# A decoder trunk on one core: the inverse's input blocks stored straight from the masked scores, their norms as four rows of a matmul, and v centred by the matmul that turns it

## The chip, the core and the metric

The kernel runs on one core of one Trainium2 chip. A core has a matrix engine (PE, whose weight loads are listed as PEld), a vector engine (DVE), a scalar engine (ACT), GpSimd (POOL) and SyncE (SP), which in this kernel does nothing but issue transfers. The transfers run on 16 DMA engines. Every engine works off its own queue in order, and semaphores hold one back for another. The metric is device microseconds for one execution; lower is better.

## What is computed

A layer of RWKV-7 time mixing, then a layer of differential attention, for a sequence of 1024 tokens and a width of 1024. All of it is float32. The change lies in the first layer, of which this part matters:

```
kk = hd(k * k_k);  kk = kk / max(sqrt(sum(kk*kk, -1)), 1e-12)     # 16 heads of 64
kmod = hd(k * (1 + (a - 1) * k_a));  decay = exp(-exp(hd(w)))
step:  sa    = state @ (-kk_t)
       state = state * decay_t + sa x (kk*ah)_t + v_t x kmod_t
       y_t   = state @ r_t
mean = mean(y, -1);  var = mean((y - mean)**2, -1)
yn = (y - mean) * rsqrt(var + GN_EPS) * ln_w + ln_b
o  = (yn + sum(rh*kmod*r_k) * vh) * silu(g)
```

The mean of y over a head is taken away by taking the mean of v over the head away beforehand, since y is linear in v.

## The kernel before, in words

**Layer one** replaces the scan over tokens by chunks of 64 tokens. A unit of work, M, is two chunks of eight heads (four pairs of heads); there are 16 of them. Each goes through these steps: `prep` (decays, the scaled k, r and a, and the masked products `pm` of every token with every other in its chunk), `invert` (the unit lower triangular system of each block of 32 tokens, by substitution on POOL), `merge` (two blocks of 32 become one of 64), `chain` (the state is carried through the two chunks) and `norm`. In the steady part, slot i runs `chain` of M[i], `norm` of M[i-1], `merge` of M[i+1], `invert` of M[i+2] and `prep` of M[i+3], with the projections of the layer (`proj_step`: 24 matmuls of 512 columns for one pair of heads and half the tokens, weights `wf` split into `wh` and `wl`) put between as filling.

**From the scores to the inverse.** `prep` writes `pm` in four DVE instructions (L502). A block of 32 tokens wants 31 rows of `pm` and, as its row 31, the squared norms of k. Before the change, a matmul (L475) with the 128x128 constant `last` sums the squares `sq` and puts the norms on every partition that is the last of a block and zero on the others; four ACT copies (L485) bring it to the tile `ab`; four DVE additions (L510) add the rows of `pm`; and one transfer (L511) stores `ab` to DRAM as `dA`, laid out [8 chunks, 4 blocks, 32 rows, 32]. A second transfer (L528) reads `dA` back as `al`, one block per partition, four times over. `invert` then takes `ni` from row 31 of `al` (L538, L539), scales `al` (L540) on DVE, starts `xx` (L542, L545) and runs 31 steps of two POOL instructions (L551, L553). The result goes out as `dX` (L556) and comes back as `qd` (L558), which `merge` turns (L576).

**v.** When `proj_step` makes v (p is 2), its result `ev` is turned by four PE transposes per step (L211), DVE sums each head (L215) and takes the mean away while it evicts (L217), and L220 stores it as `d_vc`. There are 16 such steps: eight with the first half of the tokens, early on, and eight with the second half, at the start of the steady part.

**What sets the order.** The order in which instructions stand on each engine is not the program's: a planner runs through the program with durations of its own (`Durations`) and priorities (`PRI`), and lays each engine's queue out accordingly, for layer one and the first six steps of layer two. So a change at one place can move instructions everywhere. Transfers are all issued on SP's one queue.

Of the kernel before, what the change touches and what calls it, by code (L numbers as in the profile page):

```python
# [11 lines left out]
F32 = mybir.dt.float32  # L12
# [3 lines left out]
ALU = mybir.AluOpType  # L16
AX = mybir.AxisListType
# [3 lines left out]
P = 128  # L21
# [3 lines left out]
C = 64  # L25
# [51 lines left out]
class Trunk:  # L77
# [10 lines left out]
    def start(self, lp, xnT):  # L88

        nc, tc, I = self.nc, self.tc, self.I  # L90
        const = self.const
        self.ident = const.tile([P, P], F32, name="ident")
        make_identity(nc, self.ident)
        self.par = const.tile([P, len(ROWS), KT], F32, name="par")
        self.mug = const.tile([P, 6, KT], F32, name="mug")
# [13 lines left out]
        for t0 in range(0, KT, 2):  # L109
            ms = lp.tile([P, 2], F32, name="ms")  # L110
            for i in range(2):
                sq = lp.tile([P, D], F32, name="sq", bufs=1)
# [3 lines left out]
            for i in range(2):  # L116
# [5 lines left out]
                for hf in range(2):  # L122
                    pt = self.fps.tile([P, 4, P], F32, name="fl")
# [36 lines left out]
    def proj_step(self, hf, p, pr, src, group):  # L160

        nc, I = self.nc, self.I
        sl = slice(hf * TH, (hf + 1) * TH)
        G = {"w": []}
# [31 lines left out]
        def post(k):  # L196
# [11 lines left out]
            if k == 2:  # L208
                G["pt"] = pt = self.fps.tile([P, 4, P], F32, name="fl")
                for i in range(4):  # L210
                    nc.tensor.transpose(out=pt[:, i, :], in_=G["ev"][:, i * P:(i + 1) * P], identity=self.ident)  # L211
            if k == 4:
                ptv = G["pt"].rearrange("p i (h e) -> p (i h) e", e=64)
                mn = self.evp.tile([P, 8], F32, name="mn")
                nc.vector.tensor_reduce(mn, ptv, axis=AX.X, op=ALU.add)  # L215
                vc = self.evp.tile([P, 4, P], F32, name="ev")
                nc.vector.scalar_tensor_tensor(vc.rearrange("p i (h e) -> p (i h) e", e=64),  # L217
                                               mn.unsqueeze(2).to_broadcast([P, 8, 64]), -1.0 / 64, ptv,
                                               op0=ALU.mult, op1=ALU.add)
                nc.sync.dma_start(out=self.d_vc[sl, pr * P:(pr + 1) * P].rearrange("(i p) e -> p i e", p=P), in_=vc)  # L220
# [174 lines left out]
    def wkv_open(self):  # L395
        nc, tc = self.nc, self.tc
# [26 lines left out]

        self.last = cst.tile([P, P], F32, name="last")
        nc.gpsimd.memset(self.last, 0.0)
        for o in (0, 64):
            nc.gpsimd.memset(self.last[o:o + 64, o + 31:o + 64:32], 1.0)
        self.omka = cst.tile([P, KT], F32, name="omka")
# [14 lines left out]
    def prep(self, M, following):  # L443
# [29 lines left out]
        nc.vector.tensor_tensor(ae, ae, em, op=ALU.mult)  # L473
        nps = ps.tile([P, 8, C], F32, name="sc")
        nc.tensor.matmul(nps.rearrange("p c t -> p (c t)"), lhsT=self.last, rhs=sq.rearrange("p u t -> p (u t)"), start=True, stop=True)  # L475
        yield 0
# [5 lines left out]

        ab = tp.tile([P, 8, 32], F32, name="ab")
        for b in range(4):
            nc.scalar.copy(out=ab[32 * b:32 * b + 32], in_=nps[32 * b:32 * b + 32, :, b % 2 * 32:b % 2 * 32 + 32])  # L485
        nc.gpsimd.tensor_tensor(bk[:, :, 1, :], ch(kmod), em, op=ALU.mult)
# [21 lines left out]
        for b in range(4):  # L508
            bs = slice(32 * b, 32 * b + 32)
            nc.vector.tensor_tensor(ab[bs], ab[bs], pm[bs, b // 2, :, b % 2 * 32:b % 2 * 32 + 32], op=ALU.add)  # L510
        nc.sync.dma_start(out=dA.rearrange("c x s t -> (x s) c t"), in_=ab)  # L511
        yield 0
# [217 lines left out]
    def layer1(self):  # L730
# [11 lines left out]
        self.xmp = st.enter_context(tc.tile_pool(name="xmp", bufs=XB, side="right", reuse_waits="tile"))  # L742
        self.evp = st.enter_context(tc.tile_pool(name="evp", bufs=2, side="right", reuse_waits="tile"))

        def src_of(hf):
# [592 lines left out]
```

## Time and profile before

| | us |
|---|---|
| median of 3 runs (1627.41 to 1634.28) | 1633.85 |
| the profiled execution | 1635.44 |
| its span, first to last instruction | 1633.6 |
| PE busy | 1494.4 (91%) |
| DVE busy | 1194.8 (73%) |
| ACT busy | 909.6 (56%) |
| POOL busy | 672.8 (41%) |

A row of the windows view gives, for each stretch, the length of time in which each engine was busy, the granted TensorE clock as a share of 2.4 GHz, the mean busy share of the 16 DMA engines (packets overlap on an engine, so it can be over 1) and what they moved. A row of the lines view is a group of equal instructions: line, engine, operation, what is written from what, shape, count, then busy time in us and the mean of one in ns, then the idle time just before them. In the timeline, a row is start, length, engine, line, operation and, in brackets, the idle time before it and what ended it; SPq is SP's queue, and there the length is that of the issue, not of the transfer. In the chain, a row is start, length and what.

### The profile page before, as it was taken

To read this page: it belongs to the slowest core of one execution; us is meant where nothing else is said; L and a number is where in the kernel's file an instruction comes from. 1 tells how busy PE (TensorE), PEld (TensorE's weight loads), DVE (VectorE), ACT (ScalarE), POOL (GpSimd) and SP (SyncE) were. 2 spreads that over 40 slices of the span, in tenths; PEclk is the share of its full clock that TensorE was granted. 3 is DMA by queue.
4 is the path that set the end of the run, shared out by engine and by line. 5 is a ranking of instruction groups with operands and counts; after the bars stand their busy time and mean duration, and the time that the engine had idled before them with its cause. 6 is when DMAs were issued, how large, how long until landed. Compare 5 with 4: busy or idle time off the path is not lost.

```text
span 1633.6 us, 31095 instructions
## 1 busy us (share of the span) xinstructions
PE 1494.4 (91%) x10496; PEld 1208.3 (74%) x10496; DVE 1194.8 (73%) x3119; ACT 909.6 (56%) x2095; POOL 672.8 (41%) x1685
## 2 busy tenths in 40 slices
PE   3799999988998999979869789999999999999897
PEld 3577777666776777768758567788888888888786
DVE  7745658866879798788555777887878888787764
ACT  5645565745657586655234644665565656556420
POOL 4000003856878688778656111233232333333100
PEclk8799999989999999979879789999999999999999
DMA  7654677755656567656446451211111111113231
GB/s 195 187 185 144 186 226 216 201 163 152 194 157 175 164 179 190 185 160 174 128 142 164 131 169 58 67 46 31 46 46 27 46 33 40 40 40 119 92 126 52
DMA packets 218095, 207.39 MB, mean 127 GB/s; under 512 B 78032, under 2 KB 163280, under 8 KB 217936
## 3 DMA queue, kind: packets, MB, share of 16 engines
q1 hardware_dynamic: 217936, 205.40, 42.9%
q8 instruction: 83, 1.36, 0.3%
q14 instruction: 76, 0.62, 0.1%
HBM read 147.09 MB, written 58.27 MB: 126 GB/s over the span
## 4 chain that ended last, share of the span: by engine, by line
PE 63%; DVE 14%; DMA 7%; ACT 6%; issue 5%; POOL 4%; SPq 1%; ACTq 0%; DVEq 0%; POOLq 0%
PE pj L878 6%; PE pj L877 6%; PE pj L879 6%; PE fl L192 5%; PE fl L193 5%; PE fl L194 5%; PE tr L982 4%; PE sc L940 2%; PE sc L941 2%; PE tr L970 2%; POOL xx L553 2%; POOL tm L551 2%; DMA al<-dA 1%; PE sc L498 1%; PE tr L1255 1%
## 5 line engine op out<-in xcount | busy, mean ns | idle before, releaser
L192 PE MATMUL fl<-xh,wh 128*128 128x512 f32 x512 | 212.2, 420 | 11.2 <-DVE ev L217 8.8
L877 PE MATMUL pj<-wh,xh 128*128 128x512 f32 x512 | 214.1, 418 | 0.0
L193 PE MATMUL fl<-xl,wh 128*128 128x512 f32 x512 | 209.2, 410 | 3.7 <-DVE xl L151 3.7
L553 POOL TENSOR_TENSOR xx<-xx,tm 128x60 f32<-128x60 f32 (+24 forms) x496 | 196.8, 397 | 36.4 <-DVE xx L545 0.4
L194 PE MATMUL fl<-xh,wl 128*128 128x512 f32 x512 | 209.3, 410 | 0.0
L551 POOL TENSOR_TENSOR tm<-al,xx 128x60 f32<-128x60 f32 (+24 forms) x496 | 190.2, 383 | 40.4 <-DVE xx L545 4.0
L878 PE MATMUL pj<-wh,xl 128*128 128x512 f32 x512 | 202.7, 396 | 2.6 <-DVE xl L1216 2.6
L879 PE MATMUL pj<-wl,xh 128*128 128x512 f32 x512 | 202.1, 396 | 0.0
L157 DVE TENSOR_TENSOR wl<-wf,wh 128x512 fp32r<-128x512 f32 x160 | 119.0, 748 | 80.4 <-ACT wh L156 79.5
L946 ACT ACTIVATE p<-sc,mx 128x256 f32<-128x256 f32 (+7 forms) x128 | 94.6, 741 | 142.1 <-DVE mx L945 123.1
L926 POOL CAST kh<-kh 64x128 fp32r<-64x128 f32 x128 | 45.2, 353 | 263.4 <-ACT kh L918 250.0
L156 ACT CAST wh<-wf 128x512 fp32r<-128x512 f32 x160 | 97.6, 617 | 94.1 <-PE fl L193 71.6
L192 PEld LDWEIGHTS fl<-xh,wh 128*128 128x128 f32 x512 | 98.4, 192 | 40.3 <-issue 12.4
L193 PEld LDWEIGHTS fl<-xl,wh 128*128 128x128 f32 x512 | 99.0, 193 | 29.2 <-DVE xl L151 5.2
L194 PEld LDWEIGHTS fl<-xh,wl 128*128 128x128 f32 x512 | 98.7, 193 | 24.0 <-issue 1.4
L879 PEld LDWEIGHTS pj<-wl,xh 128*128 128x128 f32 x512 | 96.8, 189 | 21.9
L878 PEld LDWEIGHTS pj<-wh,xl 128*128 128x128 f32 x512 | 97.5, 190 | 19.6 <-DVE xl L1216 4.3
L877 PEld LDWEIGHTS pj<-wh,xh 128*128 128x128 f32 x512 | 97.5, 190 | 15.4 <-ACT xh L1215 0.2
L944 DVE TENSOR_REDUCE mx<-sc 128x1 f32<-128x256 f32 (+7 forms) x128 | 95.4, 753 | 0.8
L982 PEld LDWEIGHTS tr<-v,p 128*128 128x128 f32 x576 | 74.9, 194 | 7.8 <-ACT p L972 3.2
L982 PE MATMUL tr<-v,p 128*128 128x128 f32 x576 | 76.1, 278 | 2.1 <-ACT p L972 2.1
L940 PE MATMUL sc<-kh,q 128*128 128x512 f32 (+2 forms) x192 | 70.9, 378 | 4.0 <-issue 2.1
(295 smaller groups left out, 3695.3 us busy)
## 6 DMA issues: line engine op xcount, KB each, us to landing
wf<-in_a_w_in SPq DMA_DIRECT2D x64, 512.0 KB
d_in<-ev SPq DMA_DIRECT2D x64, 256.0 KB
wf<-in_b_w SPq DMA_DIRECT2D x64, 256.0 KB
xk<-d_xn SPq DMA_DIRECT2D x40, 256.5 KB
al<-dA SPq DMA_DIRECT2D x16, 512.0 KB
wf<-in_a_w_out SPq DMA_DIRECT2D x16, 512.0 KB
p<-d_x SPq DMA_DIRECT2D x10, 512.0 KB
d_c<-cc SPq DMA_DIRECT2D x16, 260.0 KB
```

The lines of the kernel that those rows point to most:

```text
L156: self.nc.scalar.copy(out=wh, in_=wf)
L157: self.nc.vector.tensor_tensor(wl, wf, wh.bitcast(F32), op=ALU.subtract)
L192: nc.tensor.matmul(G["ps"], lhsT=wh[:, kk, :], rhs=xh, start=(k == 0), stop=False)
L193: nc.tensor.matmul(G["ps"], lhsT=wh[:, kk, :], rhs=xl, start=False, stop=False)
L194: nc.tensor.matmul(G["ps"], lhsT=wl[:, kk, :], rhs=xh, start=False, stop=(k == KT - 1))
L551: nc.gpsimd.tensor_tensor(tv, al[:, s:s + 1, s + 1:].to_broadcast([P, n, w]), xx[:, 0:n, s:s + 1].to_broadcast([P, n, w]), op=ALU.mult)
L553: nc.gpsimd.tensor_tensor(xx[:, 0:n, s + 1:], xx[:, 0:n, s + 1:], tv, op=ALU.add)
L877: nc.tensor.matmul(pf, lhsT=self.X[i][0][:, k], rhs=wh, start=(k == 0), stop=False)
L878: nc.tensor.matmul(pf, lhsT=self.X[i][1][:, k], rhs=wh, start=False, stop=False)
L879: nc.tensor.matmul(pf, lhsT=self.X[i][0][:, k], rhs=wl, start=False, stop=(k == KT - 1))
L940: nc.tensor.matmul(sc[:, b:e], lhsT=q[:, m], rhs=H["kh"][:, m, b:e], start=True, stop=False)
L982: nc.tensor.matmul(po, lhsT=at[:, b, :], rhs=H["v"][:, b, :], start=(b == 0), stop=(b == i))
```

## The change

There are two edits.

**The substitution's input.** `last` goes; a constant `pick` [128, 2, 4] takes its place, and two accumulating matmuls with four weight columns each give the norms as four rows, one for each block of a chunk, [4, 8, 32]. One ACT copy brings them to an `ab` of four partitions, and a transfer of its own stores them as row 31 of each block. The four DVE additions go. The rows 0 to 30 of each block go to DRAM from `pm` itself, in four transfers, each of 31 partitions, 8 chunks and 32 numbers. So five transfers take the place of one, with as many runs of 128 bytes in all, and `al` waits for all five.

**v centred.** A constant `less` (the identity less 1/64 in each head's block) takes the place of the identity in the four PE instructions per step, which become matmuls. What they write is centred already, so the sum and the subtraction on DVE give way to one DVE copy.

```
+        nc.gpsimd.tensor_tensor(self.less, self.less, self.ident, op=ALU.add)
...
-                    nc.tensor.transpose(out=pt[:, i, :], in_=G["ev"][:, i * P:(i + 1) * P], identity=self.ident)
+                    nc.tensor.matmul(pt[:, i, :], lhsT=G["ev"][:, i * P:(i + 1) * P], rhs=self.less, start=True, stop=True)
...
-                mn = self.evp.tile([P, 8], F32, name="mn")
-                nc.vector.tensor_reduce(mn, ptv, axis=AX.X, op=ALU.add)
...
-                nc.vector.scalar_tensor_tensor(vc.rearrange("p i (h e) -> p (i h) e", e=64),
-                                               mn.unsqueeze(2).to_broadcast([P, 8, 64]), -1.0 / 64, ptv,
-                                               op0=ALU.mult, op1=ALU.add)
+                nc.vector.tensor_copy(out=vc, in_=G["pt"])
...
-        nps = ps.tile([P, 8, C], F32, name="sc")
-        nc.tensor.matmul(nps.rearrange("p c t -> p (c t)"), lhsT=self.last, rhs=sq.rearrange("p u t -> p (u t)"), start=True, stop=True)
+        nps = ps.tile([P, 8, C], F32, name="sc")[0:4, :, 0:32]
+        for b in range(2):
+            nc.tensor.matmul(nps, lhsT=self.pick[:, b, :], rhs=ch(sq)[:, :, b * 32:b * 32 + 32], start=b == 0, stop=b == 1)
...
-        ab = tp.tile([P, 8, 32], F32, name="ab")
-        for b in range(4):
-            nc.scalar.copy(out=ab[32 * b:32 * b + 32], in_=nps[32 * b:32 * b + 32, :, b % 2 * 32:b % 2 * 32 + 32])
+        ab = tp.tile([4, 8, 32], F32, name="ab")
+        nc.scalar.copy(out=ab, in_=nps)
+        nc.sync.dma_start(out=dA[:, :, 31, :].rearrange("c x t -> x c t"), in_=ab)
...
         for b in range(4):
-            bs = slice(32 * b, 32 * b + 32)
-            nc.vector.tensor_tensor(ab[bs], ab[bs], pm[bs, b // 2, :, b % 2 * 32:b % 2 * 32 + 32], op=ALU.add)
-        nc.sync.dma_start(out=dA.rearrange("c x s t -> (x s) c t"), in_=ab)
+            bs = slice(32 * b, 32 * b + 31)
+            nc.sync.dma_start(out=dA[:, b, 0:31, :].rearrange("c s t -> s c t"), in_=pm[bs, b // 2, :, b % 2 * 32:b % 2 * 32 + 32])
```

SP's queue around the seventh unit's store of `dA` and its reading back, before; a row is line, operation, what is written from what, and the shape on the written side:

```order
L556 DMA dX<-xx 4x256x32
L204 DMA d_in_61<-ev 128x512
L168 DMA wf<-in_a_w_in 128x1024
L558 DMA qd<-dX 128x8x32
L511 DMA dA<-ab 128x8x32
L528 DMA al<-dA 128x1x1024
L441 DMA a<-d_a 128x4x128
L526 DMA d_bv<-v 128x512
L204 DMA d_in_61<-ev 128x512
L168 DMA wf<-in_a_w_in 128x1024
```

The same place on SP after the change:

```order
L205 DMA d_in_61<-ev 128x512
L169 DMA wf<-in_a_w_in 128x1024
L554 DMA dX<-xx 4x256x32
L509 DMA dA<-pm 31x8x32 x4
L556 DMA qd<-dX 128x8x32
L526 DMA al<-dA 128x1x1024
L438 DMA a<-d_a 128x4x128
L205 DMA d_in_61<-ev 128x512
L169 DMA wf<-in_a_w_in 128x1024
L524 DMA d_bv<-v 128x512
```

The one store of 128 partitions has become four of 31, which here also stand ahead of the reading of `qd`; the store of the norms (not in these rows) stands further up, and what stood behind the reading of `al` still does.

DVE's queue from the last two masks `pm` of the seventh unit on, before (`ni`, L538, stands 34 rows behind the last mask):

```order
L502 TENSOR_TENSOR pm<-sc,pmask 128x512 x2
L510 TENSOR_TENSOR ab<-ab,pm 32x256 x3
L651 COPY uv<-zu 64x4x64
L510 TENSOR_TENSOR ab<-ab,pm 32x256
L686 TENSOR_SCALAR ve<-mg 128x8
L157 TENSOR_TENSOR wl<-wf,wh 128x512
L68 TENSOR_SCALAR gn_t<-ve 128x8
```

The same place on DVE after the change:

```order
L501 TENSOR_TENSOR pm<-sc,pmask 128x512 x2
L158 TENSOR_TENSOR wl<-wf,wh 128x512
L649 COPY uv<-zu 64x4x64
L479 TENSOR_TENSOR bk<-kraw,a 64x8x64
L480 TENSOR_TENSOR bk<-kraw,a 64x8x64
L684 TENSOR_SCALAR ve<-mg 128x8
```

The additions are gone, and `ni` (L536 now) stands 27 rows behind the last mask where it stood 34 rows behind.

## Rows read from the trace of the kernel before

**Rows 1.** windows: busy us of PE, PEld, DVE, ACT, POOL; clock, DMA, GB/s

```profile
100.00:250.00 150.00, 147.94 (x662) 116.87 (x661) 88.16 (x130) 89.14 (x160) 9.88 (x28) 1.00 0.62 194
250.00:750.00 500.00, 460.75 (x4277) 355.43 (x4276) 394.63 (x852) 311.00 (x631) 367.11 (x842) 0.94 0.63 177
750.00:900.00 150.00, 124.82 (x1578) 110.92 (x1577) 91.82 (x266) 62.90 (x132) 92.82 (x254) 0.89 0.54 151
```

**Rows 2.** timeline of SP's queue at the seventh unit's store and reading

```profile
471.36 0.56 SPq L556 DMA_DIRECT2D dX<-xx  x1
...
476.30 0.37 SPq L558 DMA_DIRECT2D qd<-dX  x1
478.29 0.37 SPq L511 DMA_DIRECT2D dA<-ab  x1
480.51 0.56 SPq L528 DMA_DIRECT2D al<-dA  x1
...
486.02 0.46 SPq L168 DMA_DIRECT2D wf<-in_a_w_in  x1
```

**Rows 3.** timeline: DVE and POOL where `al` is first used

```profile
453.39 0.18 DVE L538 TENSOR_SCALAR ni<-al 128x32 f32<-128x32 f32 x1 [5.17 <-DMA al<-dA]
...
495.14 0.29 DVE L538 TENSOR_SCALAR ni<-al 128x32 f32<-128x32 f32 x1
...
471.41 0.24 POOL L551 TENSOR_TENSOR tm<-al,xx 128x31 f32<-128x31 f32 x1
```

**Rows 4.** waits: engine, line, waited for: us in total, times, longest

```profile
SPq L558 <- DMA dX<-xx: 13.3, 11, 4.3
...
SPq L528 <- DMA dA<-ab: 7.8, 5, 3.3
...
DVE ni L538 <- DMA al<-dA: 11.9, 5, 5.2
```

**Rows 5.** by line: issues of two stores, ns min/median/max, first and last start

```profile
L511 SPq DMA_DIRECT2D dA<-ab x16: 370/371/2242, 257.0 to 812.3; - x16
...
L556 SPq DMA_DIRECT2D dX<-xx x16: 533/564/572, 309.3 to 886.7; - x16
```

**Rows 6.** windows: the last `dA` and the last `dX` on their way

```profile
813.20:814.00 0.80, 0.80 (x35) 0.63 (x33) 0.60 (x3) 0.00 (x0) 0.62 (x3) 1.00 1.04 164
...
888.00:890.70 2.70, 2.70 (x46) 2.50 (x45) 1.89 (x10) 0.95 (x2) 0.47 (x1) 1.00 0.34 48
```

**Rows 7.** chain that ended last: start, us, what; two readings of `al`

```profile
261.26 10.69 DMA al<-dA
...
441.36 12.01 DMA al<-dA
```

**Rows 8.** timeline of SP's queue: the issue behind a store of `dX`

```profile
588.77 0.57 SPq L556 DMA_DIRECT2D dX<-xx  x1
589.44 2.18 SPq L168 DMA_DIRECT2D wf<-in_a_w_in  x1
```

**Rows 9.** lines: what goes on DVE and ACT, and a copy

```profile
L510 DVE TENSOR_TENSOR ab<-ab,pm 32x256 f32<-32x256 f32 x64 | 26.9, 421 | 0.9
...
L485 ACT COPY ab<-sc 32x256 f32<-32x256 f32 x64 | 23.2, 362 | 3.9 <-PE sc L475 3.2
...
L215 DVE TENSOR_REDUCE mn<-fl 128x8 f32<-128x512 f32 x16 | 11.0, 689 | 11.0 <-PE fl L211 10.9
...
L217 DVE SCALAR_TENSOR_TENSOR ev<-mn,fl 128x512 f32<-128x512 f32 x16 | 10.9, 681 | 6.0 <-DMA d_vc<-ev 5.8
...
L129 DVE COPY xnT<-fl x8: 677/684/692, 16.5 to 63.1; 128x512 f32<-128x512 f32 x8
```

**Rows 10.** lines on PE: old norms, old turn (100 to 250 us), a matmul

```profile
L475 PE MATMUL sc<-sq,last 128*128 128x512 f32 x32 | 16.8, 605 | 0.2 <-ACT sq L467 0.2
...
L211 PE MATMUL fl<-ident,ev 128*128 128x128 f32 x32 | 4.9, 275 | 0.5 <-ACT ev L203 0.5
...
L982 PE MATMUL tr<-v,p 128*128 128x128 f32 x406 | 52.7, 275 | 0.0
```

More of the change, by code (lines that the diff above doesn't have):

```diff
@@ L210, in post @@
                 for i in range(4):
-                    nc.tensor.transpose(out=pt[:, i, :], in_=G["ev"][:, i * P:(i + 1) * P], identity=self.ident)
+                    nc.tensor.matmul(pt[:, i, :], lhsT=G["ev"][:, i * P:(i + 1) * P], rhs=self.less, start=True, stop=True)
             if k == 4:
-                ptv = G["pt"].rearrange("p i (h e) -> p (i h) e", e=64)
-                mn = self.evp.tile([P, 8], F32, name="mn")
-                nc.vector.tensor_reduce(mn, ptv, axis=AX.X, op=ALU.add)
                 vc = self.evp.tile([P, 4, P], F32, name="ev")
-                nc.vector.scalar_tensor_tensor(vc.rearrange("p i (h e) -> p (i h) e", e=64),
-                                               mn.unsqueeze(2).to_broadcast([P, 8, 64]), -1.0 / 64, ptv,
-                                               op0=ALU.mult, op1=ALU.add)
+                nc.vector.tensor_copy(out=vc, in_=G["pt"])
                 nc.sync.dma_start(out=self.d_vc[sl, pr * P:(pr + 1) * P].rearrange("(i p) e -> p i e", p=P), in_=vc)
@@ L422, in wkv_open @@
         nc.gpsimd.memset(self.bones[64:P, 64:P], 1.0)
[L424 to L427, printed above, removed]
+        self.pick = cst.tile([P, 2, 4], F32, name="pick")
+        nc.gpsimd.memset(self.pick, 0.0)
+        for h in range(2):
+            for b in range(2):
+                nc.gpsimd.memset(self.pick[h * 64:h * 64 + 64, b, 2 * h + b:2 * h + b + 1], 1.0)
         self.omka = cst.tile([P, KT], F32, name="omka")
@@ L473, in prep @@
         nc.vector.tensor_tensor(ae, ae, em, op=ALU.mult)
-        nps = ps.tile([P, 8, C], F32, name="sc")
-        nc.tensor.matmul(nps.rearrange("p c t -> p (c t)"), lhsT=self.last, rhs=sq.rearrange("p u t -> p (u t)"), start=True, stop=True)
+        nps = ps.tile([P, 8, C], F32, name="sc")[0:4, :, 0:32]
+        for b in range(2):
+            nc.tensor.matmul(nps, lhsT=self.pick[:, b, :], rhs=ch(sq)[:, :, b * 32:b * 32 + 32], start=b == 0, stop=b == 1)
         yield 0
@@ L743, in layer1 @@
         self.evp = st.enter_context(tc.tile_pool(name="evp", bufs=2, side="right", reuse_waits="tile"))
+        self.less = self.evp.tile([P, P], F32, name="less", bufs=1)
+        nc.gpsimd.memset(self.less, 0.0)
+        for o in (0, 64):
+            nc.gpsimd.memset(self.less[o:o + 64, o:o + 64], -1.0 / 64)
         def src_of(hf):
```

## The prediction

> **What bounds the kernel now.** I read the windows view first, since the change touches layer one alone. From 100 to 250 us PE is busy for 147.9 of 150 us: PE sets the time there, and DVE (88.2) has room [rows 1]. From 250 to 750 us, the steady part, nothing is full and everything is close: PE 460.8, DVE 394.6 and POOL 367.1 of 500 us, the DMA engines at a share of 0.63 [rows 1]. There the time is set by who waits for whom in queues whose order is fixed. A DVE instruction whose operand is late holds up all that stands behind it, and much of that is what PE waits for. From 900 us on the work is layer two, which the change does not touch.
>
> The path that the change cuts into is: mask `pm` on DVE, store to `dA`, read back as `al`, `ni` on DVE. For the seventh unit SP issues the store at 478.29 and the reading at 480.51, when the store has landed [rows 2]; a reading takes 10.69 to 12.01 us [rows 7], so `al` is there at 491.2 to 492.5, and `ni` runs at 495.14 [rows 3]. That leaves 2.6 to 3.9 us of slack. In five of the 16 units there is none: DVE waits for `al`, 11.9 us in all, 5.17 us in the sixth unit [rows 3, 4]. So whatever makes `dA` land later by more than some 3 us stops DVE.
>
> **The change, part by part.**
>
> *DVE.* The 64 additions go, 26.9 us; in v, 16 sums (11.0 us) and 16 subtractions (10.9 us) give way to 16 copies, which I take at the 684 ns of a copy of the same shape out of PSUM, 10.9 us [rows 9]. DVE loses 26.9 + 11.0 = 37.9 us, 5.5 us of that under a PE that is full (the first half of v), where it is worth nothing.
>
> *ACT.* 64 copies of 362 ns become 16 of the same length along a partition: 23.2 us become 5.8 [rows 9]. ACT has room; nothing on the path.
>
> *PE.* A transpose of v costs 4.9 us / 32 = 153 ns. The nearest row for a full float32 matmul of that shape is the one of layer two, 52.7 us / 406 = 130 ns a record, two records a matmul, 260 ns [rows 10]. So 64 instructions cost 107 ns more each: 6.8 us, half of it, 3.4 us, where PE is full. The bound below is nothing (a transpose's price), the one above twice that. The norms: a product of 512 columns costs 16.8 us / 16 = 1.05 us [rows 10]; two of 256 columns stream as many. I take no change; were each of the four records no shorter than the 130 ns above it would be a gain of 0.5 us a unit, hidden among other PE work.
>
> *SP and POOL.* Four issues more a unit at 0.37 us each [rows 5] are 1.5 us of some 37 us between two units, and SP's rows show it idle for most of that [rows 2]. POOL gets a few small instructions at the very start, beside PE and DVE work.
>
> *The transfers, the term that decides.* There are as many blocks of 128 bytes as before, 1024, but they are shared out otherwise. The rows show the same 128 KB, in blocks of the same 128 bytes, sent in two ways. `dA`, whose slowest dimension is 128 partitions, ran with a DMA share of 1.04 and 164 GB/s: 131 KB in 0.8 us. `dX`, whose slowest dimension in DRAM is 4, ran with 0.34 and 48 GB/s: 131 KB in 2.7 us [rows 5, 6]. A third of the engines' time and 3.4 times as long: four engines with 256 blocks each (10.5 ns a block) against 16 with 64 each (12.5 ns). The reading of `al`, four copies of one source, goes the same way: 512 KB in 10.69 us is 49 GB/s [rows 7], where the whole queue moves 177 [rows 1]. So a transfer is cut into equal shares along its slowest dimension, and one of 4 gets four engines. The new stores have 31 there. No row shows such a number. 31 has no equal shares from 2 to 16, so the end I take is one engine with 248 blocks, and the next three stores in line behind it on the same engine: 992 blocks. The other end is 16 engines, unequal, and then it costs what `dA` cost.
>
> On one engine: 992 x 10.5 to 12.5 ns = 10.4 to 12.4 us. From the issue to the release of SP there were 2.22 us for `dA` and 4.94 us for `dX` [rows 2], that is 1.4 and 2.2 us beside the moving. Together 11.8 to 14.6 us, against 2.22; I take 13.3, so 11.1 us later. The issue behind a `dX` took 2.18 us [rows 8], so I expect the later three issues to be held up as well, which only shows the same time elsewhere. The additions ahead of the store fall away (4 x 0.42 us), so `al` is later by 9.4 us. The norms' store is early and small: no part in this.
>
> The Trainium skill, in "DMA: Bandwidth & Descriptors", section "Why a DMA increments its semaphore by 16 and not by 1", has a rule for this: the number of engines is the largest up to 16 that divides the slowest dimension of both sides, with 127 partitions given as one engine. By that rule 31 partitions go on one engine as well, and the shares of `dA` and `dX` above agree with it. If instead the shares were uneven, this term would be zero, and the sum would be that of the first rival.
>
> *What waits behind.* On SP, behind the reading of `al`, stand the next unit's loads, the stores of finished projections and the next weights (486.02) [rows 2]; they start up to 9 us later. On DVE, behind `ni`, stand evictions and splits that PE wants. The plan gives no more room than before: the additions are gone and `ni` stands seven rows nearer. Of 9.4 us some 3.3 are slack (above), so DVE waits about 6 us more a unit, 97 us over 16. DVE is idle for 105 of the 500 us anyway [rows 1], about 8 us a unit, in waits that can run out during the new one; I let four tenths be absorbed and put 58 us on the end. The bounds: nothing, when all is absorbed, and 16 x 9.4 = 150 us, when none is and the slack is gone.
>
> *The plan.* The order is laid out anew from the first v on. I cannot price that from rows; the 0.4% between the runs of before is my measure, 6 us either way.
>
> **Sum.** 1635.4 (the profiled execution, 1.6 us outside its span; 1.6 us above the median) + 58 + 3.4 = 1697. Against the median: **1695 us**. The relief of DVE in the steady part is in the slack and the absorption, and not counted again.
>
> **The rivals.**
>
> 1. *The shares are uneven, on many engines (faster).* Then `dA` lands as before and the additions' 1.7 us a unit come off the path. In the five units without slack that is 8 us; DVE has 32 us less in the steady part. A quarter of it, 8 us, on the end; less 3.4 us on PE: 1634 - 16 + 3 = 1621, between 1612 and 1632. For it: no row shows a dimension of 31. Against: the equal shares of rows 6. It decides by the share of the 31-row stores: near 1 rather than near 0.06.
>
> 2. *One engine, but covered (no change).* POOL takes up a unit's first step long after `ni`: the sixth unit's `ni` is at 453.39 and its first product at 471.41 [rows 3]. The inverse itself so has 18 us of room; only what stands behind `ni` on DVE and behind `al` on SP suffers. If DVE's idle time takes nearly all, 1634 + 3 - 2 = 1635, from 1627 to 1643. Against: PE is at 92%, and each long gap on DVE starves it.
>
> 3. *One engine that fills up (much slower).* All transfers pass that engine for a sixteenth of their bytes, behind 10 to 12 us of small blocks a unit; at a mean share of 0.63, with the four-engine transfers on top, it may be full. Then weights and `qd` are late too and PE's granted clock falls in the gaps (0.89 from 750 to 900 us, a mean of its levels of 2.4 and 1.2 GHz, where PE waits more [rows 1]): 16 x 9.4 = 150 us, 1634 + 150 = 1784, from 1745 up.
>
> **How the numbers follow.** The forecast, 1645 to 1745: 0.55. Rival 1: 0.17, of which 0.04 within 0.5%. Rival 2: 0.12, all within. Rival 3: 0.16. A measurement of this kernel can tell about 0.5%, 8 us, from no change. Faster by more: 0.13. Within: 0.16. Slower: 0.71. The range that holds 8 in 10 reaches down to 1625 (0.09 of rival 1 below it) and up to 1770 (0.1 of rival 3 above it). By itself the forecast has 1645 to 1745.
>
> **What would show it.** Right: a window of the four stores in which the DMA share is about a sixteenth from them alone, for 10 us or more; the reading of `al` issued 12 to 15 us after the first of them; the wait of `ni` for `al` in nearly all 16 units and some 100 us in all, from 11.9; the steady part longer by some 60 us and layer two as long as before; DVE busy some 38 us less in all; v's matmuls at 260 ns each. Wrong: a store of 31 partitions that lands in 2 to 3 us, or `ni` seldom waiting. If the stores are slow and the time is still the same, the step that failed is the absorption.

## The result, and the profile after

The changed kernel takes 1785.48 us (1777.67 to 1787.24, 4 runs) against 1632.68 us (1627.41 to 1634.28): a ratio of 1.0933, 95% interval 1.0892 to 1.0974. That is slower, as forecast, but by 153 us where 61 were forecast, and outside the range of 1625 to 1770. It is the size of the third rival, 1784. The profiled execution has a span of 1783.8 us, 150.2 more than before. From the page of after, busy time of each engine:

```profile
PE 1536.9 (86%) x10592; PEld 1240.7 (70%) x10592; DVE 1160.2 (65%) x3039; ACT 896.4 (50%) x2051; POOL 657.3 (37%) x1691
```

DVE has 34.6 us less to do, ACT 13.2 us less, and still it all takes longer. The windows view of after, with the columns and stretches of [rows 1]:

```profile
100.00:250.00 150.00, 146.67 (x671) 116.56 (x669) 82.34 (x122) 87.11 (x156) 10.38 (x29) 1.00 0.62 190
...
250.00:750.00 500.00, 405.63 (x3354) 307.41 (x3352) 288.44 (x599) 239.33 (x479) 278.82 (x660) 0.86 0.53 144
```

The stretch in which PE is full has hardly moved. In the steady part everything has thinned out: PE 460.8 to 405.6, DVE 394.6 to 288.4, POOL 367.1 to 278.8, the granted clock 0.94 to 0.86, the DMA share 0.63 to 0.53. None of the five engines has become full; all wait more. From one `ni` to the next there are 46.4 us (277.6 to 974.0 over 15 steps), where there were 37.5 (272.0 to 834.4). That is 8.9 us for each of 16 units, 142 us. The first step of the last unit's `merge` on DVE (`x1`, out of `qd`) moved from 901 to 1047 us, by 146 of the 150: layer two is as long as before.

SP's queue of after at the twelfth unit, to be held against [rows 2] (a row with x4 is four issues in a row):

```profile
767.38 8.91 SPq L509 DMA_DIRECT2D dA<-pm  x4
781.19 0.56 SPq L526 DMA_DIRECT2D al<-dA  x1
781.85 0.43 SPq L438 DMA_DIRECT2D a<-d_a  x1
782.38 0.45 SPq L235 DMA_DIRECT2D wf<-in_a_w_out  x1
782.92 3.49 SPq L205 DMA_DIRECT2D d_in<-ev  x1
```

The issues of the four stores alone hold SP for 8.9 us, and `al` is issued 13.8 us after the first. Before, the store's issue was 0.37 us and the reading came 2.2 us later. Over the 16 units the mean from the first store to the issue of `al` is 16.4 us, against 5.7. The line of the stores in after (ns, min/median/max of one issue, first and last start):

```profile
L509 SPq DMA_DIRECT2D dA<-pm x64: 235/2838/4996, 251.6 to 954.0; - x64
```

The median issue is 2.84 us: 248 blocks at 11.4 ns. In [rows 5] a store of 128 partitions took 0.37 us to issue. In the DMA records of the fifteenth unit the 992 blocks run one after another from 902.2 to 913.5 us. The windows view of after over just this stretch:

```profile
902.20:913.50 11.30, 11.30 (x126) 9.29 (x126) 10.74 (x28) 5.18 (x10) 7.58 (x19) 1.00 0.14 26
```

A share of 0.14 is one engine of 16 for the stores (0.06, somewhat more where its packets overlap) and a little else; [rows 6] has 1.04 for the same bytes before. Who waits is in the waits of after for transfers, some of the longest (engine, line, waited for: us in total, times, longest):

```profile
POOL xx L540 <- DMA dX<-xx: 86.2, 12, 14.0
ACT m L461 <- DMA a<-d_a: 66.1, 8, 13.9
DVE ni L536 <- DMA al<-dA: 58.8, 9, 12.4
ACT xm L145 <- DMA xk<-d_xn: 37.9, 9, 9.9
DVE ev L287 <- DMA ev<-in_x: 27.8, 4, 13.1
ACT wh L157 <- DMA wf<-in_a_w_in: 18.2, 4, 7.1
```

`ni` waits in 9 units, 58.8 us, from 11.9 [rows 4]. POOL's wait, until the last `xx` has been stored, was 47.9 us before. On ACT and DVE the longest is the wait for `a`, a load for a later unit that stands behind the reading of `al` on SP; before, it did not show between 250 and 900 us, and the one for `xk` (the normed input of a projection) came to 6.6 us in all. `in_x` is the input that layer one adds back at its end. The lines of after for the edit of v and the norms, beside [rows 9, 10]:

```profile
L212 PE MATMUL fl<-less,ev 128*128 128x128 f32 x128 | 18.9, 291 | 0.5 <-ACT ev L204 0.5
...
L474 PE MATMUL sc<-sq,pick 128*4 128x256 f32 x64 | 17.4, 396 | 3.9 <-ACT sq L464 2.3 <-ACT ev L204 1.6
...
L215 DVE COPY ev<-fl 128x512 f32<-128x512 f32 x16 | 11.0, 685 | 9.3 <-PE fl L212 7.4 <-DMA d_vc<-ev 1.8
```

The transposes that they replace, in before over the whole run:

```profile
L211 PE MATMUL fl<-ident,ev 128*128 128x128 f32 x64 | 11.3, 298 | 0.5 <-ACT ev L203 0.5
```

The 64 matmuls of v (two records each) cost 18.9 us, 295 ns each. The norms stream as long as before, 17.4 us against 16.8.

### The profile page after: what moved, and what is told of

Its sections match the earlier page's. It is cut to its first block, busy times and chain, and to the rows that moved or that the text cites. A ratio compares the mean times of both kernels' runs of the same rounds, so it can differ in the third digit from the quotient of the medians.

```text
span 1783.8 us, 31265 instructions
## 1 busy us (share of the span) xinstructions
PE 1536.9 (86%) x10592; PEld 1240.7 (70%) x10592; DVE 1160.2 (65%) x3039; ACT 896.4 (50%) x2051; POOL 657.3 (37%) x1691
## 4 chain that ended last, share of the span: by engine, by line
PE 42%; DMA 7%; DVE 6%; ACT 4%; issue 2%; SPq 2%; POOL 1%; DVEq 0%; ACTq 0%; POOLq 0%
PE pj L881 6%; PE pj L880 6%; PE pj L882 6%; PE tr L985 3%; PE sc L943 2%; PE tr L973 2%; PE sc L944 2%; DMA al<-dA 1%; DMA dA<-pm 1%; PE fl L281 1%; PE tr L1257 1%; PE fl L282 1%; PE fl L283 1%; PE tr L1259 1%; PE tr L1258 1%
## 5 line engine op out<-in xcount | busy, mean ns | idle before, releaser
L193 PE MATMUL fl<-xh,wh 128*128 128x512 f32 x512 | 216.9, 428 | 7.2 <-ACT xh L149 4.6
L194 PE MATMUL fl<-xl,wh 128*128 128x512 f32 x512 | 216.1, 423 | 0.5 <-DVE xl L152 0.4
L195 PE MATMUL fl<-xh,wl 128*128 128x512 f32 x512 | 213.6, 417 | 0.0
L551 POOL TENSOR_TENSOR xx<-xx,tm 128x60 f32<-128x60 f32 (+24 forms) x496 | 188.6, 380 | 36.6 <-DVE xx L543 0.4
L549 POOL TENSOR_TENSOR tm<-al,xx 128x60 f32<-128x60 f32 (+24 forms) x496 | 180.8, 365 | 42.6 <-DVE xx L543 6.5
L497 PE MATMUL sc<-ar,bk 64*128 64x128 f32 x512 | 63.3, 329 | 49.5 <-ACT ab L483 28.2
L497 PEld LDWEIGHTS sc<-ar,bk 64*128 64x128 f32 x512 | 52.4, 223 | 62.0 <-ACT ab L483 28.8
L281 PE MATMUL fl<-wh,xh 128*128 128x256 f32 x192 | 60.9, 324 | 27.7 <-DVE ev L287 18.0
```

What stands on the lines that cost most here:

```text
L193: nc.tensor.matmul(G["ps"], lhsT=wh[:, kk, :], rhs=xh, start=(k == 0), stop=False)
L194: nc.tensor.matmul(G["ps"], lhsT=wh[:, kk, :], rhs=xl, start=False, stop=False)
L195: nc.tensor.matmul(G["ps"], lhsT=wl[:, kk, :], rhs=xh, start=False, stop=(k == KT - 1))
L497: nc.tensor.matmul(pp[h][:, i, :], lhsT=bkh(h, c), rhs=ar[h * 64:h * 64 + 64, c].rearrange("p z t -> p (z t)"), start=True, stop=True)
L549: nc.gpsimd.tensor_tensor(tv, al[:, s:s + 1, s + 1:].to_broadcast([P, n, w]), xx[:, 0:n, s:s + 1].to_broadcast([P, n, w]), op=ALU.mult)
L551: nc.gpsimd.tensor_tensor(xx[:, 0:n, s + 1:], xx[:, 0:n, s + 1:], tv, op=ALU.add)
```

## The experiments

Theory A, that of the prediction: a store of 31 partitions runs on one engine, `al` is late, and DVE pays at `ni`. Rival B: the cause is something else in the change (five transfers for one, v, the order). Rival C: the shape of the stores is the cause, but the price is not paid at `ni`; it is paid by all that shares SP's queue or the busy engine. Ratios are against runs of before on the same chip; the medians of these were 1632 to 1641 us.

The table has, from each profile, the mean from the first store of `dA` to the issue of `al`, and from SP's issue records the issues of over 1 us, their number and the sum of their lengths.

| kernel | median us | ratio (95%) | store to `al`, us | long issues on SP |
|---|---|---|---|---|
| before | 1632.7 | 1 | 5.7 | 38, 96 us |
| after | 1785.5 | 1.0933 (1.0892 to 1.0974) | 16.4 | 96, 291 us |
| e1_rows32 | 1669.8 | 1.0214 (1.0187 to 1.0241) | 9.4 | 33, 92 us |
| e2_before_rows31 | 1775.7 | 1.0858 (1.0827 to 1.0889) | 16.7 | 96, 269 us |
| e5_rows32_held | 1792.8 | 1.0945 (1.0905 to 1.0986) | 13.9 | 97, 289 us |
| e9_rows32_engine | 1771.9 | 1.0802 (1.0771 to 1.0833) | 11.2 | 86, 226 us |
| e13_engine_act | 1739.3 | 1.0650 (1.0623 to 1.0677) | 10.3 | 56, 144 us |
| e10_rows32_issues | 1968.3 | 1.1980 (1.1933 to 1.2026) | 17.4 | 61, 216 us |

### Is it the shape of the stores?

**e1.** The change, with 32 partitions in each store; the norms get a row of their own, and `al` is read with 1056 numbers a block for 1024. `ni` has three buffers here, in place of four, for room.

```
-        M["dA"] = dA = self.dr.tile([8, 4, 32, 32], F32, name="dA")
+        M["dA"] = dA = self.dr.tile([8, 4, 33, 32], F32, name="dA")
...
-            bs = slice(32 * b, 32 * b + 31)
+            bs = slice(32 * b, 32 * b + 32)
```

> The changed kernel with 32 partitions in each of the four stores instead of 31 (the norms go to a 33rd row of the block, and the reading takes 33 rows); nothing else differs but a smaller pool for ni. Theory A, 31 rows have no equal share but one engine: each issue behind the first falls from 2.8 us to about 0.4, the stores land 2 to 4 us after the first issue instead of 13 to 18, the steady part gets its 37 us a unit back, and the kernel takes 1610 to 1640 us. Theory B, the loss of 150 us is from the new plan, the five transfers in place of one and the matmuls of v: the time stays above 1720 us.

1669.76 us. The line of the stores in e1, in the columns as above:

```profile
L509 SPq DMA_DIRECT2D dA<-pm x64: 303/442/2588, 252.2 to 831.2; - x64
```

The issues are short again and 116 us are gone, with one partition more in each store. So the shape is most of it; some 35 us are left.

**e6.** The change, with each store cut into 30 partitions and 1.

```
-            bs = slice(32 * b, 32 * b + 31)
+            for o, n in ((0, 30), (30, 1)):
+                bs = slice(32 * b + o, 32 * b + o + n)
```

> The changed kernel with each store of 31 partitions cut into one of 30 and one of 1. By the rule of equal shares, 30 partitions go on 15 engines (16 blocks each) and 1 on one engine (8 blocks): the stores land in 3 to 6 us and the time falls to 1660 to 1700 us, near that of 32 rows. If only powers of two share evenly, 30 goes on two engines, 120 blocks each, and four of them take 5 to 6 us more: 1700 to 1740 us. If a store over one engine is due to the count being under 32, it stays at 1780 us.

1659.99 us, ratio 1.0129 (1.0091 to 1.0166). The same 31 rows, in twice as many transfers, and no worse than with 32 (1.0214). So it is not the bytes and not the number of transfers.

**e2.** Before, with its additions, its norms and its v; only the store of `ab` is cut, as the change cuts it.

```
-        nc.sync.dma_start(out=dA.rearrange("c x s t -> (x s) c t"), in_=ab)
+        nc.sync.dma_start(out=dA[:, :, 31, :].rearrange("c x t -> x c t"), in_=ab[31::32])
+        for b in range(4):
+            nc.sync.dma_start(out=dA[:, b, 0:31, :].rearrange("c s t -> s c t"), in_=ab[32 * b:32 * b + 31])
```

> The kernel before, with its one store of 128 partitions cut into the shapes of the changed kernel: four of 31 partitions and one of four, all from ab; the additions, the old norms and the old v stay. Theory A (the shape of the stores alone): 1750 to 1800 us, with 13 to 18 us from the first store to the reading of al. Theory B (new plan, v and norms): under 1670 us.

1775.69 us: the cut of the store alone does it, 140 us on a kernel that is otherwise untouched. **e14**, the same store cut into four of 32 partitions, is the control:

```
-        nc.sync.dma_start(out=dA.rearrange("c x s t -> (x s) c t"), in_=ab)
+        for b in range(4):
+            nc.sync.dma_start(out=dA[:, b].rearrange("c s t -> s c t"), in_=ab[32 * b:32 * b + 32])
```

> The kernel before with its one store of 128 partitions cut into four of 32, all of the same sums. It tests what is left in e1 and e7 (25 to 30 us over before) when the stores are shared out. Theory 'four issues and four landings in place of one, and the order that follows from it': 1650 to 1670. Theory 'the norms (their own store and their place) or the masks as the source': within 8 us of before.

1640.63 us, ratio 1.0045 (1.0027 to 1.0063). So 31 for 32 partitions costs 8.1% here, and four issues for one half a percent. (e2 has the norms' store as a fifth, which e14 has not; e1 and the change both have it, and there it is 7.2%.) The Trainium skill, "DMA: Bandwidth & Descriptors", section "Why a DMA increments its semaphore by 16 and not by 1", takes as the number of engines the largest up to 16 that divides the slowest dimension of both sides; that would be 1 engine for 31, 15 for 30, 16 for 32. The times of e2, e6 and e14 agree, and so do the 992 blocks one after another; how many engines 30 got, no row shows.

### Where is it paid?

**e5.** e1, with four stores of 31 partitions a unit added behind the reading of `al`. They write a DRAM tile that nobody reads; nothing waits for them.

```
+        dB = self.dr.tile([8, 4, 32, 32], F32, name="dB")
+        for b in range(4):
+            nc.sync.dma_start(out=dB[:, b, 0:31, :].rearrange("c s t -> s c t"), in_=bkt[32 * b:32 * b + 31, 0, :, 0:32])
```

> The variant with 32 rows in a store, with four more stores of 31 partitions (to a DRAM tile that nobody reads, from bkt) placed about the reading of al. They hold SP and the one DMA engine as long as the changed kernel's own stores do, while al itself comes early. Theory A (what costs is SP's queue and the one engine, so the next unit's loads): most of the loss returns, 1740 to 1800 us. Theory B (what costs is that al is late and ni stops DVE, as the prediction had it): within 25 us of the 1670 us of the variant without them.

1792.75 us: the whole loss is back. The waits of e5:

```profile
ACT m L461 <- DMA a<-d_a: 97.4, 10, 21.0
ACT wh L157 <- DMA wf<-in_a_w_in: 50.4, 9, 14.3
DVE ni L539 <- DMA al<-dA: 35.9, 9, 9.3
```

`ni` waits less than in after (35.9 for 58.8) and the kernel is no faster. The waits for `a` and for the weights have grown in its place. That speaks for rival C. But here too `al` is issued later than in e1 (13.9 us for 9.4), so e5 alone does not rule `ni` out; e9 goes further.

**e9.** Is it SP, held by long issues, or the engine? e1 with two added stores a unit, also of 31 partitions, but in blocks of 4 KB: as long on the engine, with 62 blocks instead of 992.

```
+        dB = self.dr.tile([2, 31, 1024], F32, name="dB")
+        for i in range(2):
+            nc.sync.dma_start(out=dB[i], in_=bkt[0:31].rearrange("p h c t -> p (h c t)"))
```

> The kernel of e1_rows32 (stores of 32 partitions, 1669.8 us) with two added stores a unit of 31 partitions by 4 KB, from bkt to a DRAM tile that nobody reads. The DMA records should show them on one engine for some 10 us a unit, like the four stores of after, but as 62 large blocks instead of 992 of 128 bytes, so that SP's issues should stay short (0.4 to 0.6 us). Theory 'the one engine is full' (every transfer passes this engine for a sixteenth of its bytes and is late by what stands in front there): most of the loss is back, 1735 to 1790. Theory 'SP's queue is held' (issues of some 2.8 us while 248 blocks are taken up; the loads behind them are issued late): no more than 15 us over e1, 1665 to 1685.

1771.91 us, 102 over e1. The DMA records show the 62 blocks one behind the other, in 11.2 us in the fourteenth unit. Two waits of e9:

```profile
ACT m L461 <- DMA a<-d_a: 96.4, 11, 18.4
DVE ni L539 <- DMA al<-dA: 19.1, 6, 7.5
```

`ni` waits 6 us more than in e1 (12.9), `al` is issued 1.8 us later, and 102 us are lost. In the chain that ended last, `a` has 18.0% of the time from 250 to 1050 us and `al` 2.7%. So one busy engine can cost this much with `al` hardly late: rival C. How the change's own loss divides between `al` and the others is not shown by this; in its chain over the same stretch the four stores have 2.9%, `al` 3.0, `a` 1.4.

SP's queue of e9 at the twelfth unit:

```profile
765.59 0.57 SPq L526 DMA_DIRECT2D al<-dA  x1
766.26 0.74 SPq L529 DMA_DIRECT2D dB<-bkt  x2
767.74 2.63 SPq L438 DMA_DIRECT2D a<-d_a  x1
771.44 4.83 SPq L435 DMA_DIRECT2D cc<-d_c  x1
776.32 4.77 SPq L524 DMA_DIRECT2D d_bv<-v  x1
781.13 0.49 SPq L235 DMA_DIRECT2D wf<-in_a_w_out  x1
```

The added stores are issued in 0.37 us each, as expected. But now the next three issues are held, 2.6 to 4.8 us each, though those are transfers of 128 partitions. (The fourth behind them is short again.) My two theories were not apart: the busy engine holds SP, only later in the queue.

**e13.** So the same two stores, issued from ACT's queue, right behind the ACT copy that makes `bkt`:

```
-            nc.sync.dma_start(out=dB[i], in_=bkt[0:31].rearrange("p h c t -> p (h c t)"))
+            nc.scalar.dma_start(out=dB[i], in_=bkt[0:31].rearrange("p h c t -> p (h c t)"))
```

> The kernel of e9 with its two added stores (31 partitions by 4 KB, to a DRAM tile that nobody reads) issued from ACT's queue and not from SP's. The one engine is as busy as in e9 (1771.9), but these blocks no longer stand in SP's own queue. Theory 'SP's issues are held because their blocks queue behind the small or long ones on this one engine in the same queue': SP's long issues go, and the time is near e1, 1665 to 1700. Theory 'the engine itself is the limit, whichever queue feeds it': 1735 to 1790.

1739.30 us: in the range of the second theory, yet 33 us under e9. SP's queue of e13 behind the reading of the seventh unit, with the added stores on their way from 529:

```profile
526.29 0.56 SPq L526 DMA_DIRECT2D al<-dA  x1
526.95 0.44 SPq L169 DMA_DIRECT2D wf<-in_a_w_in  x1
531.50 0.37 SPq L438 DMA_DIRECT2D a<-d_a  x1
532.23 0.32 SPq L524 DMA_DIRECT2D d_bv<-v  x1
```

Here SP's issues are short, and over the run the long ones fall from 226 to 144 us (92 in e1). ACT is not held either: its issues of `dB` take 202 to 471 ns. Still 70 of e9's 102 us stay. The waits of e13:

```profile
ACT m L461 <- DMA a<-d_a: 57.3, 9, 11.8
DVE ni L539 <- DMA al<-dA: 33.5, 8, 8.3
ACT xm L145 <- DMA xk<-d_xn: 25.0, 5, 16.8
```

Loads whose issue was not held are late as well: eight of the nine waits for `a` follow an issue of 0.37 to 0.42 us and end 10.0 to 16.8 us behind it, where in e1 the three behind a short issue end after 8.4 to 11.4. The DMA records show how: from 375.1 to 378.1 us they are 18 blocks of 512 bytes from SP's queue and 17 of 4 KB from ACT's, one by one in turn (and one of 4 bytes). That fits transfers that have all landed but for their part on the busy engine, which gets one block through between two of the added store. So both are at work. With the other queue about a third of e9's added loss goes (by the ratios a quarter); the rest is at most the engine's, since SP still has 52 us more of long issues than in e1. That is two kernels, each in its own order, which can make 10 us (below), and how it divides for the change's blocks of 128 bytes was not measured. The Trainium skill, same page, section "Queues, rings and completion order", says that SP and ACT have rings of their own on the same 16 engines, and that an engine takes turns between them: e13 agrees in both, by the blocks in turn from 375.1 us on and by the 70 us that stay though SP is freer.

**e10.** The other way round: SP held, no engine filled. e1 with 24 stores a unit of 16 numbers each.

```
+        dB = self.dr.tile([24, 16, 1], F32, name="dB")
+        for i in range(24):
+            nc.sync.dma_start(out=dB[i], in_=bkt[0:16, 0, 0, i:i + 1])
```

> The kernel of e1_rows32 with 24 added stores a unit of 16 partitions by one number, from bkt to a DRAM tile that nobody reads: 24 issues of some 0.37 us hold SP's queue for about 9 us a unit, and the 16 engines get 24 tiny blocks each. Theory 'SP's queue is held': the loss is back, 1735 to 1790. Theory 'the one engine is full': 1665 to 1695.

1968.26 us, far over what I expected. A held SP is dear by itself, but the size says little: the added stores also wait, on SP, for the reading of `al` (58.5 us in 10 waits) and for one another (44.9 us in 29), and the next `al` comes late (`ni` waits 95.5 us). It shows that a held SP can cost more than the change does; it doesn't divide the change's loss.

### The parts, and what is left at 32 partitions

**e3** is before with the edit of v alone (and two buffers for `ni` and `ve` in place of four, for room), **e4** the change with the old v:

```
-                    nc.tensor.transpose(out=pt[:, i, :], in_=G["ev"][:, i * P:(i + 1) * P], identity=self.ident)
+                    nc.tensor.matmul(pt[:, i, :], lhsT=G["ev"][:, i * P:(i + 1) * P], rhs=self.less, start=True, stop=True)
```

> The kernel before with the edit of v alone (ni and ve have two buffers instead of four, for room). Theory A: PE pays 3 us where it is full, DVE gains 11 us where it matters little: 1626 to 1640 us. Theory B (v carries a part of the loss): over 1650 us.

> The changed kernel with the old turn and centring of v. Theory A: the whole loss stays, 1770 to 1800 us. Theory B (v carries a part of it): under 1750 us.

1650.43 us, ratio 1.0097 (1.0070 to 1.0124), and 1772.07 us, 1.0840 (1.0808 to 1.0872). **e7** is e1 with the old v:

> The variant with 32 rows in a store, with the old turn and centring of v. If v's edit costs 13 to 16 us of itself (e3_v_alone against before, the changed kernel against e4_store_alone): 1650 to 1660 us. If that cost is the new plan's: as likely above 1670 us as under it. The additions' 27 us of DVE and four store issues in place of one remain in it: under 1630 us would show that the edit of the stores is worth something.

1664.83 us, 1.0147 (1.0116 to 1.0178). In all three places the new v is slower, by 0.7 to 1.0%: 11 to 16 us, where 3.4 were forecast. (e3 has the fewer buffers besides; the other two pairs differ in v alone.)

**e8 and e12** measure the order alone. They are before with one number of the planner changed in each, the same work:

```
-LATER, BACK, MOVING, SLOWER, SCAN = 1000, 4000, 1.3, 105, 550
+LATER, BACK, MOVING, SLOWER, SCAN = 1000, 4000, 1.3, 106, 550
...
+LATER, BACK, MOVING, SLOWER, SCAN = 1020, 4000, 1.3, 105, 550
```

> The kernel before with nothing changed but one constant of the planner: it takes a POOL instruction for 1 ns longer (SLOWER 106 for 105). The work is the same; the order differs from the first slots on. If the plan is worth 6 us either way, as the prediction had it: 1627 to 1641 us. If a new plan by itself costs what v's edit seemed to cost: 1645 to 1665 us.

> The kernel before with one number of the planner changed (LATER 1020 for 1000): the same instructions in an order that differs somewhat. The prediction put 6 us either way on the order; e8, another such change, gave 0.999. If the order alone can make the 25 us that are left in e7, this is off by over 1%: below 1618 or over 1650. If not, within 0.5% of before.

1640.21 us, ratio 0.9990 (0.9970 to 1.0010), and 1650.51 us, 1.0061 (1.0042 to 1.0081). So a new order can cost 10 us, and the new v's 11 to 16 us are partly within that.

What remains is why e7, with the old v, is still 1.5% over before. **e11** moves the issue of the norms' store behind the masks:

```
-        nc.sync.dma_start(out=dA[:, :, 32, :].rearrange("c x t -> x c t"), in_=ab)
         nc.gpsimd.tensor_tensor(bk[:, :, 1, :], ch(kmod), em, op=ALU.mult)
...
+        nc.sync.dma_start(out=dA[:, :, 32, :].rearrange("c x t -> x c t"), in_=ab)
         for b in range(4):
```

> The kernel of e7_rows32_no_v (stores of 32 partitions, old turn of v, 1664.8 us) with the issue of the norms' store moved from behind the copy ab to behind the last mask, just ahead of the four stores. It tests what is left of the loss when the stores are shared out (some 25 us over before). Theory 'SP stands at the norms' store, waiting for ACT's ab, and what is behind it is late': back by 10 to 25 us, 1640 to 1655. Theory 'it is the number of issues, or the order that the plan comes out with': within 6 us of 1665.

1660.83 us, 1.0133 (1.0096 to 1.0170): no more than 4 us. **e15** issues all five stores from ACT's queue:

```
-            nc.sync.dma_start(out=dA[:, b, 0:32, :].rearrange("c s t -> s c t"), in_=pm[bs, b // 2, :, b % 2 * 32:b % 2 * 32 + 32])
+            nc.scalar.dma_start(out=dA[:, b, 0:32, :].rearrange("c s t -> s c t"), in_=pm[bs, b // 2, :, b % 2 * 32:b % 2 * 32 + 32])
```

> The kernel of e7_rows32_no_v with its five stores a unit issued from ACT's queue, so that SP neither issues them nor stands at them; SP still stands at the reading of al until they have landed. Theory 'SP's time is what the rest of the loss pays for': 10 to 25 us less than 1665, so 1640 to 1655. Theory 'ACT stands at the masks instead and what is behind it is late': 1665 or more.

1667.04 us, 1.0221 (1.0187 to 1.0255): nothing gained, though ACT may now pay for standing at the masks. **e16** makes the norms as before:

```
+        nc.tensor.matmul(nps.rearrange("p c t -> p (c t)"), lhsT=self.last, rhs=sq.rearrange("p u t -> p (u t)"), start=True, stop=True)
...
+        nc.sync.dma_start(out=dA[:, :, 32, :].rearrange("c x t -> x c t"), in_=ab[31::32])
```

> The kernel of e7_rows32_no_v (1664.8 us) with the norms made as before: the product of 512 columns, four copies on ACT, and their store from four rows of ab. The masks still go straight to four stores of 32 partitions. Theory 'the new norms make what is left of the loss': within 8 us of before, 1630 to 1645. Theory 'the masks as the source of the stores, without the additions, make it': 1655 to 1675.

1661.90 us, 1.0161 (1.0118 to 1.0203): not the norms. **e17** keeps the new norms and copies the masks on DVE into one tile, from which the stores go:

```
+            nc.vector.tensor_copy(out=am[bs], in_=pm[bs, b // 2, :, b % 2 * 32:b % 2 * 32 + 32])
-            nc.sync.dma_start(out=dA[:, b, 0:32, :].rearrange("c s t -> s c t"), in_=pm[bs, b // 2, :, b % 2 * 32:b % 2 * 32 + 32])
+            nc.sync.dma_start(out=dA[:, b, 0:32, :].rearrange("c s t -> s c t"), in_=am[bs])
```

> The kernel of e7_rows32_no_v (1664.8 us) with the masks copied by DVE into one tile of 128 rows (four copies a unit, where before has four additions) from which the four stores of 32 partitions go. The new norms stay. Theory 'the masks as the source make what is left': 1630 to 1645. Theory 'the new norms make it': 1655 to 1680.

1643.01 us, 1.0069 (1.0043 to 1.0095): about half of e7's 1.5% is gone. **e18** is e7 with `SLOWER` 106 for 105, the edit of e8:

> The kernel of e7_rows32_no_v (1664.8 us) with one number of the planner changed (SLOWER 106 for 105, as in e8), so that the same instructions come out in another order. Theory 'the 20 us that e7 and e16 have over e17 are an accident of the order': it moves by 10 us or more, to 1655 or below. Theory 'the masks as the source cost it, whatever the order': within 8 us of 1665.

1674.35 us, 1.0221 (1.0186 to 1.0256): another order of e7 is not better. So neither the norms nor their place makes it, and moving the issues off SP does not help. The five kernels with 32 partitions and the old v that store straight from the masks (e7, e11, e15, e16, e18) lie at 1.3 to 2.2%; the two that store from a gathered tile (e14, e17) at 0.5 and 0.7%. That points to the masks as the source, but does not show it: e17 is one kernel in one order, and an order alone moved 0.6% (e12) and 0.7% (e18 against e7). What of that source would cost the time is open too: the packets are as long, and SP stands longer for e17's copies (29.9 us) than for e7's masks (14.3). The copy of e17 puts back the DVE work that the change had saved at this place. No kernel here is faster than before.

## Why the prediction was wrong

**One engine: right.** 992 blocks in 11.3 us were forecast at 10.4 to 12.4.

**How late `al` is: right.** From the first store to the reading 11.1 us more were forecast; measured are 16.4 against 5.7 us, 10.7 more. (The 2.22 us of the seventh unit, from which the forecast set out, is short for a unit, so the 12 to 15 us that it gave as a sign came out as 16.4.) The 1.7 us for the additions was not measured by itself.

**The price: the step that failed.** The term is the 58 us for what `al`'s lateness costs. The prediction took the 9.4 us to `ni`, let 3.3 of them go into slack, and of the 97 us of waits let four tenths go into DVE's idle time. It looked for waits of some 100 us at `ni`, in nearly all units: there are 58.8 us, in 9. And a unit is 8.9 us longer, nearly all of the lateness, although `ni` often doesn't wait. Its waits grew by 46.9 us, so that even with nothing absorbed they would make, by an estimate from these waits, 47 of the 153 us. The slack and the idle time belong to DVE, and most of the price is not paid there: e9 loses 102 us with `ni` waiting 6 us more, and e5, with less waiting at `ni` than after, loses as much as the change. What waits in its place are users of `a`, `xk`, `wf` and `in_x`, transfers that pass the same engine or stand behind it on SP; for these the sum had nothing. The bound above of the term, 150 us with nothing absorbed, is the size that came, but by another path than the one it was worked out for.

**The held issues: noticed, and given no price.** From [rows 8] the prediction expected the later issues to be held and wrote that this "only shows the same time elsewhere". It shows where the cost is: SP's long issues went from 96 to 291 us, 137 of it the four stores themselves. The paragraph on what waits behind named the right transfers and put no term into the sum for them.

**Rival 3, with 0.16, is nearest to what happened,** in size (1784) and in kind: weights and loads late, the granted clock down, 0.94 to 0.86 in the steady part. The size is in part luck: it is 16 times the lateness of `al`, and not worked out from an engine that is full. The rival said that the engine "may be full"; e9 and e13 show that some 11 us a unit on one engine are enough. PE's busy time grew by 42.5 us, of which v's matmuls account for 7.6; the lower clock fits the rest, but what it adds to the time was not measured apart.

**The small terms.** v's matmuls: 119 ns more each (295 against 11.3 us / 64 = 177 for the transposes), forecast 107; but the edit costs 11 to 16 us on the end, not 3.4. DVE 34.6 us less, forecast 37.9; ACT 13.2, forecast 17.4. The order was priced at 6 us either way; e12 alone has 10. That the stores go straight from the masks was not seen as a possible cost. By the ratios: e14 0.5%, e17 0.7, e7 1.5, e1 2.1, after 9.3; so of the 153 us some 117 are 31 for 32 partitions. The rest, split the same way, would be 11 for v, 13 for the masks as the source, and 11 for the cut into four and the norms, but each of these is about what an order alone can make.

**Layer two as long as before: right.**

## What to carry to other kernels

Before a store is cut, look at its slowest dimension: here 32 partitions, or 30 and 1, cost 1 to 2% and 31 cost 9%, and a spare row cost less than a row left out. A transfer that lands on one engine is not priced at its reader's slack but as time taken from every transfer that passes this engine or stands behind it on the issuing queue; where the plan is as tight as here, count it in full: 10.7 us later made 8.9 us a unit. And a copy that gathers rows before the store may be worth more than the DVE time that it takes, as e17 suggests.

## What was new of the hardware

A transfer that runs on one engine can be issued in 0.37 us and hold others. In e9, behind the reading of `al` and 62 blocks of 4 KB on one engine, the next loads and stores, of 128 partitions, took 2.6 to 4.8 us to issue; in e1, without these blocks, the load of `a` right behind an `al` took 0.47 us (at 499.04). With blocks of 128 bytes the transfer holds its own followers, 2.84 us for each 248 blocks in after.

Such a hold also stands behind `al` and `dX`, which by the shares and rates of [rows 6, 7] ran on a part of the engines, and it was there before the change. Where SP issues `dX` right behind an `al`, the next issue is held, in before four times, for 7.6 to 9.7 us:

```profile
775.49 0.57 SPq L528 DMA_DIRECT2D al<-dA  x1
776.11 0.55 SPq L556 DMA_DIRECT2D dX<-xx  x1
776.75 9.74 SPq L239 DMA_DIRECT2D wf<-in_a_w_out  x1
```

In after the norms' store, of four rows, once stands at that place:

```profile
917.00 0.60 SPq L526 DMA_DIRECT2D al<-dA  x1
917.69 0.56 SPq L554 DMA_DIRECT2D dX<-xx  x1
918.35 10.85 SPq L484 DMA_DIRECT2D dA<-ab  x1
```

The prediction had said that this store has no part in it. That is the longest of its 16 issues in the trace; their median is 0.36 us. The prediction went by the 2.18 us behind a `dX` alone [rows 8]; the longer ones, in the same trace of before, would have told it that a held SP has a price.
